# Split activations placed 8 or 16 bytes off a 128-byte line, another place in each stage

## The chip, the cores and the metric

The program runs on one core of one Trainium2 chip. The metric is the device time of one execution in microseconds. A core has TensorE (PE in the profile; its weight loads are shown apart, as PEld), VectorE (DVE), ScalarE (ACT), GpSimd (POOL) and SyncE (SP), which here issues most DMAs.

## The reference

Two transformer blocks run one after the other on 256 tokens of width 1024, all in float32. What is left out below are the gates, masks and scans of each mixer.

```python
def first_block(x, mem, ...):                  # depth 1
    h = h + concat(mlstm(norm(h)), window_attention(norm(h))) @ w_out
    h = h + memory_cross_attention(norm(h), norm(mem), ...)
    h = h + peer_ffn(norm(h), ...)             # 16384 experts, 16 of them per head and token
    return rmsnorm(h, g_final)

def second_block(x, ...):                      # depth 2: even_mixer, then odd_mixer
    h = h + mixer(norm(h))
    h = h + conv_ffn(norm(h))                  # (silu(conv(u)) * v) @ w_down, width 2816
```

The PEER stage is computed here densely: every one of the 16384 experts is multiplied with all tokens, and the coefficients of those not chosen are zero.

## The kernel before

Activations lie feature-major in SBUF: a tile of 128 partitions by 8 blocks of 256 tokens, `[P, 8, T]`. A float32 product is made of three matmuls in the type fp32r. Each operand is split into a high part (`hi`, rounded to fp32r) and a low part (`lo`, what is left), and the sum of high by high, high by low and low by high is accumulated in PSUM (`mm3`, `out_step`). So every matmul of a projection reads a 128x128 block of a weight tile as its stationary operand and 256 tokens of an activation tile, 1024 bytes in each partition, as its moving operand; in `proj_a` the parts are exchanged, and 512 columns of a weight tile are moving.

`weight` brings one weight tile of 512 KB at a time: a DMA on SP into `raw`, `hi` on ACT, `lo` on DVE. The tiles rotate through three to six buffers. One weight tile feeds 24 matmuls of 256 columns: 8 blocks by 3 products.

The stages follow one another: mix (mLSTM and window attention), cross, peer (queries, then 128 tiles of `down`, then 128 tiles of `up` with the coefficients as moving operand), even, ffn0, odd, ffn1. The split activations of a stage come from one of four places:

- `Norm(i)`: the tiles `xh` and `xl` (in the pool `xq`, or `xq2` after the peer stage), or `uh` and `ul` in the pool `xu` for i = 1 (memory) and 3 (peer queries). The 256-column projections read them as moving operand.
- `pair()`: `oh` and `ol`, the input of an output projection in mix, cross, even and odd.
- `peer`: `x.hi` and `x.lo` for the `down` tiles; `u1` for the coefficients of the `up` tiles (`u3` in the program, shown as `u` in the profile).
- `ffn`: `uh` and `ul`, six buffers of 256 tokens each.

Instructions are issued in the order in which the program is recorded; a scheduling layer adds the waits and assigns addresses in the pools. A pool's tiles lie one behind the other, so a pool's start is moved by a small unused tile ahead of it:

```python
    def skip(self, pool, nbytes):
        t = pool.tile([P, nbytes // 4], F32, tag="skip", name="skip", bufs=1)
        self.nc.gpsimd.memset(t, 0.0)
```

In the built program every weight tile (`raw`, `hi`, `lo`) begins at a multiple of 128 bytes. All split activations begin 64 bytes past such a multiple, except those of ffn1 (`Norm(8)`, and `uh`, `ul` of `ffn(1)`), which begin at a multiple.

Of the kernel before, what the change touches and what calls it, by code (L numbers as in the profile page):

```python
# [11 lines left out]
F32R = mybir.dt.float32r  # L12
# [9 lines left out]
P = 128  # L22
T = 256
# [124 lines left out]
    return o  # L148


class Norm:
    early, late = 1, 3

    def __init__(self, b, h, i, pool, tag="x", rpool=None, off=0):
        self.b, self.h = b, h
        self.g = b.g[:, i]
        self.hi, self.lo = [b.placed(pool, F32R, tag + n, off) for n in "hl"]
        self.r = self.R = None
        self.rpool = rpool or b.sp
        self.tag, self.pieces, self.queue = tag, 0, []  # L160
        self.squares = {}
# [211 lines left out]
class Builder:  # L373
# [14 lines left out]
            kw["side"] = side  # L388
        return ctx.enter_context(self.tc.tile_pool(name=name, bufs=bufs, **kw))

    def placed(self, pool, dtype, tag, off):
        if not off:
            return pool.tile([P, 8, T], dtype, tag=tag, name=tag)
        t = pool.tile([P, 8 * T + 32], dtype, tag=tag, name=tag)
        return t[:, off:off + 8 * T].rearrange("p (k t) -> p k t", k=8)

    def skip(self, pool, nbytes):
        t = pool.tile([P, nbytes // 4], F32, tag="skip", name="skip", bufs=1)
        self.nc.gpsimd.memset(t, 0.0)
# [211 lines left out]

    def pair(self):
        o = Pair()
        o.hi = self.op.tile([P, 8, T], F32R, tag=self.ot + "h", name="oh")
        o.lo = self.op.tile([P, 8, T], F32R, tag=self.ot + "l", name="ol")
        return o

    def consts(self, names, arr):
# [29 lines left out]
    def build(self):  # L648
        nc = self.nc
        st = self.stages or ALL  # L650
        last = st[-1]

        def norm(i):
            if i == 3:
                return lambda: Norm(self, self.h, i, self.xu, "u")
            return lambda: Norm(self, self.h, i, self.xq, off=16 if i == 8 else 0)

        def store():
            return Store(self, self.h)

        def final():
            x = Final(self, self.h, self.xq)
            return Finish(self, x) if last == "peer" else x

        self.c = {}
        with ExitStack() as ctx:
            self.sp = self.pool(ctx, "small", bufs=2)
            self.psp = self.pool(ctx, "psum", space=PSUM)
            self.xu = self.pool(ctx, "xu", bufs=1)
            self.skip(self.pool(ctx, "gap"), 64)  # L670
            base = self.pool(ctx, "w0")
            late = ExitStack()
            cq = ExitStack()
            self.skip(self.pool(cq, "gapq", side="right"), 32)
            self.xq = self.pool(cq, "xq", side="right")
            cx = ExitStack()
            self.h = self.pool(cx, "h1", side="right").tile([P, 8, T], F32, tag="h", name="h")
            self.g = self.sp.tile([P, 9, 8], F32, tag="g", name="g", bufs=1)
            self.act_set("silu_and_others")
            nc.scalar.dma_start(self.g, self.A["g_cols"].rearrange("p (i k) -> p i k", i=9))  # L680
            self.ident = self.sp.tile([P, P], F32, tag="ident", name="ident", bufs=1)

            def load_x(i):
                nc.sync.dma_start(self.h[:, 2 * i:2 * i + 2], self.A["x"][:, 2 * i:2 * i + 2])

            load_x(0)
            self.one = self.sp.tile([P, 1], F32, tag="one", name="one", bufs=1)
            nc.vector.memset(self.one, 1.0)
            x = None
            self.wn = 0  # L690
            cw = ExitStack()
            self.wps = [(base, 3), (self.pool(cw, "w1"), 2)]
            with ExitStack() as c1:
                self.cp = self.pool(c1, "c_early")
                self.skip(self.pool(c1, "gapp"), 64)
                self.xp = self.op = self.pool(c1, "xp")
                self.ot = "o"
                if "mix" in st:
                    x = norm(0)()
                    x.split(0)  # L700
                    first = self.weight(self.A["w_in_t"][0], parts=2)
                    for i in range(1, 4):
                        load_x(i)
                        x.split(i)
                    nc.scalar.dma_start(self.ident, self.A["c_ident"])
                    for i in range(4):
                        x.squared(i)
                    x = self.mix(x, first, store if last == "mix" else norm(2))
                else:
                    for i in range(1, 4):  # L710
                        load_x(i)
                    nc.scalar.dma_start(self.ident, self.A["c_ident"])
                if "cross" in st:
                    x = self.cross(x, store if last == "cross" else norm(3), "mix" not in st)
            if "peer" in st:
                x = x or norm(3)().both()
                spill = self.pool(ctx, "spill", space=bass.MemoryType.DRAM).tile([P, 8, T], F32, name="spill")
                x = self.peer(x, base, cw, cx, cq, late, spill, final)
                cx = ExitStack()
                self.wn, self.free = 3, 3  # L720
            else:
                cw.close()
                self.wn = 0
                self.cp = self.pool(late, "c_late", side="right")
                self.consts(LATE, "c_late")
            with ExitStack() as c2:
                self.wps = [(base, 3), (self.pool(c2, "w2"), 3)]
                self.op, self.ot = self.xu, "u"
                if "even" in st:
                    if "peer" not in st:  # L730
                        x = norm(5)().both()
                    x = self.even(x, store if last == "even" else norm(6))
                if "ffn0" in st:
                    x = x or norm(6)().both()
                    x = self.ffn(x, 0, store if last == "ffn0" else norm(7))
                if "odd" in st:
                    x = x or norm(7)().both()
                    x = self.odd(x, store if last == "odd" else norm(8))
                if "ffn1" in st:
                    x = x or norm(8)().both()  # L740
                    self.ffn(x, 1, store)
            late.close()
            cx.close()
            cq.close()
# [336 lines left out]
    def peer(self, xu, base, cw, cx, cq, late, spill, nxt):  # L1081
        nc, A = self.nc, self.A
        mm = nc.tensor.matmul
        with ExitStack() as ctx:
# [1 line left out]
            store = dp.tile([P // 2, P, 2 * T], F32, name="store")  # L1086
            nc.sync.dma_start(spill, self.h)
            x = Pair()
            x.hi = self.xq.tile([P, 8, T], F32R, tag="xh", name="xh")
            x.lo = self.xq.tile([P, 8, T], F32R, tag="xl", name="xl")  # L1090
            work = []
            clock = [0.0, 0.0]

# [33 lines left out]
            for hd in range(8):  # L1127
                before, q = q, rt.tile([P, 2, T], F32, tag="q", name="q")
                for half in range(2):
# [4 lines left out]
                    k = 2 * hd + half - xu.late + 1  # L1134
# [8 lines left out]
            u1 = self.xu.tile([P, 8, T], F32, tag="uh", name="u1")  # L1143
# [80 lines left out]
            nc.sync.dma_start(self.h, spill)  # L1224
            self.cp = self.pool(late, "c_late", side="right")
            self.consts(LATE, "c_late")
            u1 = self.xu.tile([P, 8, T], F32R, tag="uh", name="u3")
            order = [j for j in range(0, P, 2) if j >= kept] + [j for j in range(GA, P, 2) if j < kept]
            order += [j for j in range(0, GA, 2) if j < kept]
            coef = {}  # L1230
# [293 lines left out]
    def ffn(self, x, l, nxt):  # L1524
        nc, A = self.nc, self.A
        with ExitStack() as ctx:
            mp = self.pool(ctx, "ffn%d" % l)
            self.skip(mp, 32 if l else 96)
            mt = self.pool(ctx, "ffnt%d" % l, bufs=6)
            cw = mp.tile([P, FT, 4], F32, name="cw")  # L1530
            nc.sync.dma_start(cw, A["ffn_conv"][l].rearrange("p (f j) -> p f j", j=4))
# [1 line left out]
            def step(f):  # L1533
                u = mt.tile([P, T], F32, tag="u", name="u", bufs=3)

                def ev_u(ps):
                    w = mt.tile([P, T], F32, tag="w", name="w", bufs=2)
                    nc.vector.tensor_mul(w, ps, x.R)
                    nc.scalar.activation(u, w, AF.Identity, scale=cw[:, f, 2:3], bias=cw[:, f, 3:4])
                    for j in (1, 2):  # L1540
                        nc.vector.scalar_tensor_tensor(u[:, j:], w[:, :T - j], cw[:, f, 2 - j:3 - j], u[:, j:],
                                                       op0=ALU.mult, op1=ALU.add)
                    nc.scalar.activation(u, u, AF.Silu)
                    nc.vector.tensor_mul(u, u, x.R)

                self.run(self.proj_b(x, A["ffn_up"][l, f], ev_u, self.tp))
                uh = mt.tile([P, T], F32R, tag="uh", name="uh")
                ul = mt.tile([P, T], F32R, tag="ul", name="ul")

                def ev_v(ps):  # L1550
                    nc.vector.tensor_mul(u, u, ps)
                    self.split(uh, ul, u)

                self.run(self.proj_b(x, A["ffn_up"][l, FT + f], ev_v, self.tp))
                return uh, ul

            after = Lazy(nxt)

            ahead = [step(0), step(1)]

            def steps(f):
# [189 lines left out]
```

## Time and profile before

| | |
|---|---|
| median of 3 runs | 1741.6 us (1729.73 to 1748.4) |
| the profiled execution | 1739.33 us |
| its span, first to last instruction | 1737.6 us |
| PE busy | 1683.0 us, 97% |
| DVE, ACT, POOL busy | 1241.1, 873.8, 89.1 us |

The difference between the profiled execution and its span, 1.7 us, lies outside the instructions. The three runs differ by 1.1%. A busy PE means that at least one matmul was in flight: matmuls overlap, and the profile shows for each a duration that is longer than the distance to the next one. So the rate of the matmuls is read from the distances of their starts, or from how many there are in a stretch.

### The profile page before, as it was taken

Reading aid. Unit: us, or ns where it says so; the run is one execution under the profiler, and the core shown is the slowest. Engines: PE = TensorE matmul, PEld = TensorE weight load, DVE = VectorE, ACT = ScalarE, POOL = GpSimd, SP = SyncE. Lnnn points to the kernel's source line nnn. Section 1 sums busy time; section 2 is a strip of 40 time slices with the busy share of each in tenths; the row PEclk is TensorE's granted clock in tenths of the full one; section 3 lists DMA queues with packets and bytes.
Section 4 is the critical chain, followed back from the end, with each engine's and each line's share of the span. In section 5 each row is a group of like instructions: output and inputs, shape, how many; then the busy total and the mean of one; then the engine's idle time right before and its main releaser. Section 6 shows DMA issues by size and latency. Waiting matters only on the chain.

```text
span 1737.6 us, 33082 instructions
## 1 busy us (share of the span) xinstructions
PE 1683.0 (97%) x13220; PEld 1602.0 (92%) x13220; DVE 1241.1 (71%) x2309; ACT 873.8 (50%) x1358; POOL 89.1 (5%) x246
## 2 busy tenths in 40 slices
PE   7999999999999999999999999899999999999999
PEld 6879889999999999989999999678999987799998
DVE  6686559998798985678555556686777765677775
ACT  6445345545455554444444446464555454455543
POOL 1011010000000000000000000401100010210000
PEclk9999999999999999999999999999999999999999
DMA  7434454577555655889655556443455544345551
GB/s 263 152 104 147 146 172 131 187 236 260 175 186 199 194 196 188 309 289 299 190 189 186 185 189 210 157 135 110 162 192 186 191 159 155 102 162 190 188 188 62
DMA packets 97516, 318.03 MB, mean 183 GB/s; under 512 B 11841, under 2 KB 13505, under 8 KB 96850
## 3 DMA queue, kind: packets, MB, share of 16 engines
q1 hardware_dynamic: 89154, 301.39, 53.1%
q10 hardware_dynamic: 8208, 14.52, 2.2%
q8 instruction: 104, 1.70, 0.4%
q14 instruction: 50, 0.41, 0.1%
HBM read 299.36 MB, written 16.52 MB: 182 GB/s over the span
## 4 chain that ended last, share of the span: by engine, by line
PE 70%; DVE 7%; DMA 3%; POOL 2%; issue 2%; ACT 1%; SPq 0%; POOLq 0%; DVEq 0%; ACTq 0%
PE tp L440 11%; PE tp L441 11%; PE tp L442 11%; PE acc L582 8%; PE acc L583 8%; PE acc L584 8%; PE acc L440 3%; PE acc L441 3%; DMA u<-store 3%; PE acc L442 3%; DVE lo L431 2%; PE tp L1192 1%; PE tp L1193 1%; DVE ga L1244 1%; DVE w L1345 1%
## 5 line engine op out<-in xcount | busy, mean ns | idle before, releaser
L430 ACT ACTIVATE hi<-raw 128x1024 fp32r<-128x1024 f32 (+1 forms) x533 | 560.2, 1057 | 660.8 <-PE tp L441 246.6
L431 DVE TENSOR_TENSOR lo<-raw,hi 128x1024 fp32r<-128x1024 f32 (+1 forms) x533 | 646.7, 1219 | 309.5 <-ACT hi L430 309.2
L440 PE MATMUL tp<-xh,hi 128*128 128x256 f32 x1680 | 476.7, 284 | 0.6 <-ACT u L1207 0.6
L441 PE MATMUL tp<-xl,hi 128*128 128x256 f32 x1680 | 471.8, 281 | 0.0
L442 PE MATMUL tp<-xh,lo 128*128 128x256 f32 x1680 | 471.1, 280 | 0.6 <-DVE lo L431 0.6
L442 PEld LDWEIGHTS tp<-xh,lo 128*128 128x128 f32 x1680 | 317.1, 189 | 0.8 <-DVE lo L431 0.8
L440 PEld LDWEIGHTS tp<-xh,hi 128*128 128x128 f32 x1680 | 317.0, 189 | 0.8 <-ACT u L1207 0.8
L441 PEld LDWEIGHTS tp<-xl,hi 128*128 128x128 f32 x1680 | 317.2, 189 | 0.0
L583 PE MATMUL acc<-u,hi 128*128 128x256 f32 x1024 | 288.4, 282 | 5.6 <-DVE u L436 5.6
L584 PE MATMUL acc<-u,lo 128*128 128x256 f32 x1024 | 288.2, 281 | 1.4 <-DVE lo L431 1.4
L582 PE MATMUL acc<-u,hi 128*128 128x256 f32 x1024 | 287.9, 281 | 0.0
L583 PEld LDWEIGHTS acc<-u,hi 128*128 128x128 f32 x1024 | 193.0, 188 | 6.4 <-DVE u L436 6.4
L584 PEld LDWEIGHTS acc<-u,lo 128*128 128x128 f32 x1024 | 196.9, 192 | 1.8 <-DVE lo L431 1.8
L582 PEld LDWEIGHTS acc<-u,hi 128*128 128x128 f32 x1024 | 193.0, 189 | 0.0
L440 PE MATMUL acc<-hi,xh 128*128 128x512 f32 (+1 forms) x256 | 103.5, 406 | 1.6 <-ACT y L479 1.6
L441 PE MATMUL acc<-lo,xh 128*128 128x512 f32 (+1 forms) x256 | 101.7, 397 | 0.5 <-DVE lo L431 0.5
L442 PE MATMUL acc<-hi,xl 128*128 128x512 f32 (+1 forms) x256 | 101.1, 395 | 0.0
L582 PE MATMUL acc<-uh,hi 128*128 128x256 f32 x352 | 98.3, 280 | 0.1
L583 PE MATMUL acc<-ul,hi 128*128 128x256 f32 x352 | 98.1, 279 | 0.0
L584 PE MATMUL acc<-uh,lo 128*128 128x256 f32 x352 | 98.1, 279 | 0.0
L457 POOL TENSOR_SCALAR rs_g<-rs_m 128x2 int32<-128x2 int32 (+2 forms) x20 | 10.2, 510 | 1263.8 <-DVE fq L296 810.3
L582 PE MATMUL acc<-oh,hi 128*128 128x256 f32 x256 | 73.1, 285 | 0.0
(436 smaller groups left out, 2801.8 us busy)
## 6 DMA issues: line engine op xcount, KB each, us to landing
raw<-down SPq DMA_DIRECT2D x128, 512.0 KB, 3.7
raw<-up SPq DMA_DIRECT2D x128, 512.0 KB, 4.4
raw<-ffn_up SPq DMA_DIRECT2D x88, 512.0 KB, 3.5
raw<-ffn_down SPq DMA_DIRECT2D x44, 512.0 KB, 3.4
raw<-even_in SPq DMA_DIRECT2D x28, 512.0 KB, 4.4
store<-u ACTq DMA_DIRECT2D x55, 256.0 KB, 3.4
u<-store SPq DMA_DIRECT2D x55, 256.0 KB, 4.7
raw<-odd_in SPq DMA_DIRECT2D x24, 512.0 KB, 3.5
```

Of the source, the lines that this page charges most:

```text
L430: nc.scalar.activation(hi[:, c], raw[:, c], AF.Copy)
L431: nc.vector.tensor_sub(lo[:, c], raw[:, c], hi[:, c].bitcast(F32))
L440: mm(out, lh, rh, start=start, stop=False)
L441: mm(out, lh, rl, start=False, stop=False)
L442: mm(out, ll, rh, start=False, stop=stop)
L582: mm(out, wh[:, cs], oh, start=start and j == 0, stop=False)
L583: mm(out, wh[:, cs], ol, start=False, stop=False)
L584: mm(out, wl[:, cs], oh, start=False, stop=stop and j == 1)
L1192: mm(o, p1[:, b, :, e], hi[:, b, :, e], start=True, stop=False)
L1193: mm(o, p1[:, b, :, e], lo[:, b, :, e], start=False, stop=True)
L1244: nc.vector.tensor_mul(src, src, a)
L1345: nc.vector.match_replace(out=w, in_to_replace=val[:, :8], in_values=s, imm_value=-3e38)
```

## The change

A helper `placed` makes a tile with 32 spare elements (128 bytes) and returns the part that begins `at` bytes in. The pools that hold split activations now begin at a multiple of 128 bytes (`xq2` after the peer stage: 64 past one, as before), and a table gives each stage its own place. Weights stay at multiples of 128. The instructions on PE, DVE, ACT and SP are the same in number, shape and order; on GpSimd one memset of a `skip` tile is gone and two have another size.

Since each of the two tiles of a pair is 128 bytes longer, `xl` lies 8320 bytes behind `xh` (8192 before in mix, cross and peer; 8320 before already in the later stages).

What the built program then has for each stage, in bytes past a multiple of 128 (matmuls with 256 moving columns):

| stage | tile | matmuls | before | after |
|---|---|---|---|---|
| mix projections | Norm 0 | 216 | 64 | 56 |
| memory projections | Norm 1 | 192 | 64 | 104 |
| mix and cross output | pair "o" | 384 | 64 | 88 |
| cross queries | Norm 2 | 192 | 64 | 40 |
| peer queries | Norm 3 | 384 | 64 | 24 |
| peer down | x | 3072 | 64 | 16 |
| peer up | u1 | 3072 | 64 | 48 |
| even and odd output | pair "u" | 384 | 64 | 120 |
| ffn0 up | Norm 6 | 1056 | 64 | 80 |
| ffn0 down | uh, ul | 528 | 64 | 112 |
| odd, one tile | Norm 7 | 24 | 64 | 112 |
| ffn1 up | Norm 8 | 1056 | 0 | 72 |
| ffn1 down | uh, ul | 528 | 0 | 8 |

In `proj_a`, where the activations are stationary (816 matmuls with 512 moving weight columns), they begin at 56 (mix), 104 (memory), 80 (even) and 112 (odd) instead of 64. Some float32 tiles of mix and cross move by 64 bytes with their pools.

```diff
+NORM_AT = {0: 56, 1: 104, 2: 40, 3: 24, 5: 16, 6: 16, 7: 48, 8: 8}
+PAIR_AT = {"o": 88, "u": 120}
+EXPERT_AT = 16
+COEF_AT = 48
+FFN_AT = (112, 8)
+LINE = 32
+
+
+def placed(pool, n, dtype, tag, at, **kw):
+    t = pool.tile([P, n + LINE], dtype, tag=tag, name=tag, **kw)
+    return t[:, at // 4:at // 4 + n]
...
-    def __init__(self, b, h, i, pool, tag="x", rpool=None, off=0):
+    def __init__(self, b, h, i, pool, tag="x", rpool=None):
...
-        self.hi, self.lo = [b.placed(pool, F32R, tag + n, off) for n in "hl"]
+        self.hi, self.lo = [placed(pool, 8 * T, F32R, tag + n, NORM_AT[i]).rearrange("p (k t) -> p k t", k=8)
+                            for n in "hl"]
...
-        o.hi = self.op.tile([P, 8, T], F32R, tag=self.ot + "h", name="oh")
-        o.lo = self.op.tile([P, 8, T], F32R, tag=self.ot + "l", name="ol")
+        o.hi, o.lo = [placed(self.op, 8 * T, F32R, self.ot + n, PAIR_AT[self.ot]).rearrange("p (k t) -> p k t", k=8)
+                      for n in "hl"]
...
-            return lambda: Norm(self, self.h, i, self.xq, off=16 if i == 8 else 0)
+            return lambda: Norm(self, self.h, i, self.xq)
...
+            self.skip(self.pool(ctx, "gap"), 64)
             self.xu = self.pool(ctx, "xu", bufs=1)
-            self.skip(self.pool(ctx, "gap"), 64)
...
-            self.skip(self.pool(cq, "gapq", side="right"), 32)
+            self.skip(self.pool(cq, "gapq", side="right"), 96)
...
-                self.skip(self.pool(c1, "gapp"), 64)
...
-            x.hi = self.xq.tile([P, 8, T], F32R, tag="xh", name="xh")
-            x.lo = self.xq.tile([P, 8, T], F32R, tag="xl", name="xl")
+            x.hi, x.lo = [placed(self.xq, 8 * T, F32R, n, EXPERT_AT).rearrange("p (k t) -> p k t", k=8)
+                          for n in ("xh", "xl")]
...
-            u1 = self.xu.tile([P, 8, T], F32R, tag="uh", name="u3")
+            u1 = placed(self.xu, 8 * T, F32R, "uh", COEF_AT).rearrange("p (k t) -> p k t", k=8)
...
-            self.skip(mp, 32 if l else 96)
+            self.skip(mp, 32)
...
-                uh = mt.tile([P, T], F32R, tag="uh", name="uh")
-                ul = mt.tile([P, T], F32R, tag="ul", name="ul")
+                uh, ul = [placed(mt, T, F32R, n, FFN_AT[l]) for n in ("uh", "ul")]
```

## Rows read from the trace of the kernel before

**Rows 1.** The page: span, and busy time of each engine

```profile
span 1737.6 us, 33082 instructions
PE 1683.0 (97%) x13220; PEld 1602.0 (92%) x13220; DVE 1241.1 (71%) x2309; ACT 873.8 (50%) x1358; POOL 89.1 (5%) x246
```

**Rows 2.** Busy time by stretch: peer down, peer up (three), ffn0, ffn1

```profile
core 0: us, PE busy (x) PEld busy (x) DVE busy (x) ACT busy (x) POOL busy (x), PEclk, DMA share, GB/s
302.00:452.00 150.00, 148.75 (x1259) 148.14 (x1258) 139.47 (x454) 76.49 (x115) 0.00 (x0) 1.00 0.66 220
700.00:750.00 50.00, 50.00 (x427) 50.00 (x426) 34.67 (x43) 22.65 (x27) 0.00 (x0) 1.00 0.90 316
750.00:802.00 52.00, 46.95 (x401) 45.92 (x399) 39.94 (x53) 22.03 (x25) 0.00 (x0) 1.00 0.89 301
825.00:1050.00 225.00, 225.00 (x1913) 225.00 (x1912) 121.07 (x121) 105.13 (x120) 0.00 (x0) 1.00 0.60 188
1250.00:1400.00 150.00, 150.00 (x1292) 150.00 (x1291) 109.14 (x164) 77.37 (x109) 0.00 (x0) 1.00 0.58 189
1570.00:1720.00 150.00, 150.00 (x1274) 150.00 (x1273) 107.28 (x161) 75.52 (x107) 0.00 (x0) 1.00 0.52 166
```

**Rows 3.** PE in order of time in peer up, at 900 us

```profile
start us, us, engine line op out<-in xcount [idle before <-releaser]
899.79 0.28 PE L583 MATMUL acc<-u,hi 128*128 128x256 f32 x1
...
900.85 0.28 PE L583 MATMUL acc<-u,hi 128*128 128x256 f32 x1
```

**Rows 4.** PE in order of time in peer up, at 797 us

```profile
796.78 0.28 PE L582 MATMUL acc<-u,hi 128*128 128x256 f32 x1
...
797.46 0.28 PE L582 MATMUL acc<-u,hi 128*128 128x256 f32 x1
```

**Rows 5.** Groups of PE and PEld from 825 to 1050 us (busy us, mean ns)

```profile
L582 PE MATMUL acc<-u,hi 128*128 128x256 f32 x638 | 179.3, 281 | 0.0
L584 PEld LDWEIGHTS acc<-u,lo 128*128 128x128 f32 x638 | 122.5, 192 | 0.0
L582 PEld LDWEIGHTS acc<-u,hi 128*128 128x128 f32 x637 | 119.6, 188 | 0.0
```

**Rows 6.** Groups of PE and PEld from 792 to 800 us

```profile
L582 PE MATMUL acc<-u,hi 128*128 128x256 f32 x24 | 6.6, 276 | 0.0
L584 PEld LDWEIGHTS acc<-u,lo 128*128 128x128 f32 x24 | 4.5, 188 | 0.0
```

**Rows 7.** Groups of PE from 1250 to 1400 us, ffn0: up, then down

```profile
L440 PE MATMUL tp<-xh,hi 128*128 128x256 f32 x294 | 82.5, 281 | 0.0
L582 PE MATMUL acc<-uh,hi 128*128 128x256 f32 x136 | 37.6, 277 | 0.0
```

**Rows 8.** Groups of PE from 1570 to 1720 us, ffn1: up, then down

```profile
L441 PE MATMUL tp<-xl,hi 128*128 128x256 f32 x288 | 81.2, 282 | 0.0
L582 PE MATMUL acc<-uh,hi 128*128 128x256 f32 x137 | 38.4, 280 | 0.0
```

**Rows 9.** Waits, longest first in total, from 700 to 810 us

```profile
ACT hi L430 <- DMA raw<-up: 38.2, 21, 3.1
DVE ga L1244 <- DMA u<-store: 18.3, 13, 2.9
```

**Rows 10.** Float32 matmuls of mix on four places 8 bytes apart, by line (min/median/max ns)

```profile
L865 PE MATMUL tp<-vx,pm x8: 275/275/275, 58.5 to 78.0; 128*128 128x129 f32 x8
```

**Rows 11.** Groups of PE by shape, whole span: 512 moving weight columns

```profile
L442 PE MATMUL acc<-hi,xl 128*128 128x512 f32 x240 | 96.7, 403 | 0.0
L442 PE MATMUL acc<-hi,ul 128*128 128x512 f32 x32 | 12.7, 396 | 0.0
```

More of the change, by code (lines that the diff above doesn't have):

```diff
@@ L389, in pool @@
         return ctx.enter_context(self.tc.tile_pool(name=name, bufs=bufs, **kw))
[L391 to L395, printed above, removed]
     def skip(self, pool, nbytes):
```

## The prediction

> **What bounds the kernel now.** I began with the page's busy shares: PE is busy for 1683.0 of 1737.6 us [rows 1], so nothing on another engine matters unless it holds PE up. Then I cut the span into stretches by stage. In peer up (825 to 1050 us), ffn0 and ffn1 PE has no idle time at all, and in peer down it has 1.25 us of 150; DVE, the next engine, is at 139.47 of 150 there and below three quarters elsewhere, the granted clock is 1.00, its upper level of 2.4 GHz, and the DMA engines are at 0.52 to 0.66 [rows 2]. There the time is the number of matmuls times the distance from one to the next. The exception lies from 700 to about 810 us, where the DMA share is 0.90 and PE loses 5 us in the second of the two stretches, waiting behind weights and reloaded activations [rows 2, 9].
>
> The next view is PE in order of time, read for the distances of starts. At 900 us nine steps take 1.06 us, 117.8 ns each [rows 3]. At 797 us, same line, same tiles, same places, six steps take 0.68 us, 113.3 ns each [rows 4]. 256 columns at 2.4 GHz would take 106.7 ns; 113.3 is 17/16 of that, and 117.8 is another 4.5 ns. So this matmul has **two rates** without any difference in the program. The group views show the same by their means, 281 ns against 276, which tells me how to find the rate of any stage: 276 is the fast one, 281 the slow one [rows 5, 6]. With the slow rate one load of three, that of `lo`, takes 192 ns instead of 188 [rows 5, 6]. The loads of the next block's weights run while a matmul streams, so I read the 4.5 ns as moving operand and weight load getting into each other's way, as a matter of where each stands in its stream when the other begins.
>
> The stages then sort themselves. Peer up is slow except for some 300 matmuls between 757 and 801 us; ffn0 up is slow (281), ffn0 down fast (277), both with activations at 64; ffn1, with activations at 0, is slow in both parts (282 and 280) [rows 5 to 8]. By counts, ffn0 takes 150 us for 1292 matmuls, 116.1 ns, and ffn1 150 us for 1274, 117.7 ns [rows 2].
>
> **The change part by part.** Nothing is added or removed on PE, DVE, ACT or SP, and no wait moves; one small memset less on GpSimd, which is busy 5% [rows 1], costs nothing. What can change is the cost of reading a moving operand that begins elsewhere, and the meeting of the two streams.
>
> Meeting of the streams, best case: every matmul at 113.3 ns. Slow now are the 3072 of peer down, about 2770 of peer up, 1056 of ffn0 up and 1584 of ffn1: 8482 matmuls by 4.5 ns are 38 us. The matmuls from 700 to 750 us (427, 2 us) gain nothing, since DMA at 0.90 is the next limit there; in peer down DVE has 10.5 us left in 150 [rows 2] and the gain is 5.7, so it just fits. That leaves 36 us. The shorter stages of mix, cross, even and odd hold about 1000 more slow matmuls, 4.5 us, mostly hidden under their waits for other engines. The 512-column matmuls of `proj_a`, with the activation as the load, differ by 403 against 396 ns between stages [rows 11]: 816 by 7 ns, at most 6 us.
>
> Meeting of the streams, worst case known: the matmuls that are fast now (528 in ffn0 down, some 300 in peer up, and about 700 in the short stages) fall to the slow rate: 1500 by 4.5 ns, 7 us more.
>
> Which of these holds for the new places no row can say, because the trace has only 64 and 0. What it says is that at 64 both rates occur and a stage keeps the one that it fell into until PE stalls, and that 0 gives no better than the slow one. Twelve different places, 8 or 16 bytes off the ones that are known, most likely give again a mixture. I take the present sum with a little of either end.
>
> A moving operand that begins off an even boundary may also need one more piece read. The nearest row for this is the only one with starts 8 bytes apart: float32 matmuls on `vx`, at four places, take 275 ns at minimum, median and maximum [rows 10]. But a plain float32 matmul runs at half the column rate, so it has slack that an fp32r one has not. I bound the price from below with nothing, by that row. From above: 113.3 ns is 17/16 of the ideal; if this means that data comes in pieces of 64 bytes and each takes 17 cycles instead of 16, then 1024 bytes off a 64-byte boundary touch 17 pieces instead of 16, and a matmul takes 17 by 17 cycles, 289 or 120.4 ns. I take the lower end, by the row, and keep the other as a rival.
>
> ACT and DVE write the split tiles at the new places. That is on no path: from 825 to 1050 us DVE is busy 121.07 us and ACT 105.13 of 225 [rows 2]; they would have to become almost twice as slow before PE waited. In peer down DVE could take 7%.
>
> Sum: the profiled execution is 1739.33 us, 2 us under the median of the three runs; the difference is inside their spread of 1.1%, and I make no correction. With no cost of reading and a mixture of rates as now, from the slow rate everywhere (+7) to a third of the possible gain (-14), the time is 1725 to 1746. I take 1738.
>
> **The rivals.** First, **the mixture stays** (the forecast): 1725 to 1746. For it: both rates occur at one and the same place, so the place alone doesn't choose. Against it: at 0 there is no run of the fast rate as long as those at 64, so the place does matter somewhat.
>
> The Trainium skill goes further: "TensorE: Matmul & The Clock Gate", section "Step-by-step: what each phase is for", says that PE has two independent SBUF read ports, one for the streamed operand and one for the weight loads, and that loading the next weights steals no read bandwidth from the running matmul. By that rule no place would matter, and the time would be the present one, 1739. The trace does not agree in full: a load of 192 instead of 188 ns and a matmul of 281 instead of 276 at the same addresses [rows 5, 6] show that the two do touch.
>
> Second, **the new places take the streams apart**: the fast rate nearly everywhere, 36 us less, with the short stages and `proj_a` up to 45: 1694 to 1703. If half of the large stages get it, about 1720. For it: three quarters of the matmuls are slow now, so there is far more to win than to lose, and a place that is neither 0 nor 64 could shift the meeting for good. Against it: it would have to hold for places as different as 16 and 48 in the two stages that carry most.
>
> Third, **one more piece per matmul**, on the other side: 120.4 ns wherever an activation is the moving operand. The 8482 slow ones lose 2.6 ns each, 22 us, the 1500 fast ones 7.1 ns, 11 us: 1772. It is worth over 1% as soon as about half of the matmuls pay it; were the meeting to come on top (another 4.5 ns), it would go beyond 1800. For it: the 17/16 is there in the fast rate too, where nothing else explains it, so the supply of data is the limit, and a supply limit is what extra pieces would make worse. Against it: 64 and 0 give no hint of a boundary, and pieces may be smaller than 64 bytes. With pieces of 32 bytes there are 33 for 32, 116.9 ns, and the time is within 1% of the present.
>
> "SBUF — State Buffer", section "Specifications (TRN2)", of the Trainium skill gives a line as 16 bytes, with a penalty for each new one. By that only the 8-byte places, 3336 matmuls, touch one line more, 65 for 64, an estimate of 1.8 ns each and 6 us in all: 1745. No run here shows it.
>
> **How the numbers follow.** Chances: the mixture stays 0.45, taken apart in at least half of the large stages 0.26, one more piece 0.29. About 1% is what these runs can tell from no change. Below 1724 lie the second rival and a little of the first: 0.28. Above 1759 lies most of the third: 0.28. Between them is 0.44. The range that leaves out 2 in 10: its lower end at 1704, which keeps the partial forms of the second rival; its upper end at 1776, which keeps the third without the meeting on top.
>
> **What would show it.** In the changed kernel's profile, the distances of starts, or the mean of each group, decide stage by stage: 276 ns in peer down, peer up, ffn0 up and ffn1 would be the second rival; 281 in most and 276 in some, the forecast; about 283 or more in all large stages, the third. If the cost comes from a boundary, the 8-byte stages (ffn1, peer queries) differ from the 16-byte ones (peer, ffn0). DVE and ACT means should stay where they are; if `lo` or the split of an activation grew, that would be a cost that I put at nothing. The forecast is wrong if a single place in peer down or peer up, 3072 matmuls each, moves by more than 6 ns.

## The result: slower by 0.8%

| | before | after |
|---|---|---|
| median of 18 runs | 1734.36 us (1728.44 to 1748.4) | 1749.0 us (1745.21 to 1757.15) |
| the profiled execution | 1739.33 us | 1751.94 us |
| ratio, 95% interval | | 1.0083 (1.0064 to 1.0102) |

The time lies inside the range of the prediction and within 1% of the present one, but on the other side of it: a hair faster was forecast (1738 against 1739.33), and it is measurably slower.

The page of the changed kernel, span and busy times; [rows 1] answer to it:

```profile
span 1750.2 us, 33081 instructions
PE 1699.2 (97%) x13220; PEld 1619.3 (93%) x13220; DVE 1242.1 (71%) x2309; ACT 874.1 (50%) x1358; POOL 88.3 (5%) x245
```

PE is busy 16.2 us longer, the span is 12.6 us longer, so PE is idle 3.6 us less (54.6 us before, 51.0 after): a little of the loss hides in waits for other engines; these are one execution of each kernel. DVE and ACT are the same to 1 us. The two costliest groups of these engines, from the page (engine, operation, names, count, busy us, mean ns):

```profile
L439 ACT ACTIVATE hi<-raw 128x1024 fp32r<-128x1024 f32 (+1 forms) x533 | 560.4, 1057 | 671.3 <-PE tp L450 257.1
L440 DVE TENSOR_TENSOR lo<-raw,hi 128x1024 fp32r<-128x1024 f32 (+1 forms) x533 | 646.5, 1218 | 312.8 <-ACT hi L439 312.5
```

Before they took 1057 and 1219 ns. The whole change is in the rate of PE. By stretch, as [rows 2]:

```profile
302.00:452.00 150.00, 149.39 (x1265) 148.87 (x1264) 140.31 (x460) 76.50 (x117) 0.00 (x0) 1.00 0.68 220
825.00:1050.00 225.00, 225.00 (x1904) 225.00 (x1903) 121.83 (x122) 104.98 (x120) 0.00 (x0) 1.00 0.59 188
1250.00:1400.00 150.00, 150.00 (x1268) 150.00 (x1267) 107.44 (x161) 75.69 (x107) 0.00 (x0) 1.00 0.58 185
1570.00:1720.00 150.00, 150.00 (x1256) 150.00 (x1255) 106.88 (x159) 75.02 (x106) 0.00 (x0) 1.00 0.55 178
```

Peer down counts 1265 matmuls where 1259 stood only because PE is idle less in its window, 0.61 us instead of 1.25; per busy time both give 118.1 ns. In the same time peer up gets 1904 matmuls instead of 1913, ffn0 1268 instead of 1292, ffn1 1256 instead of 1274; a matmul of ffn1 now takes 150 us / 1256 = 119.4 ns, of ffn0 118.3. The granted clock is 1.00 in each, its upper level of 2.4 GHz, as before. Groups of ffn0 from 1250 to 1400 us, up and down, as [rows 7]:

```profile
L449 PE MATMUL tp<-xh,hi 128*128 128x256 f32 x279 | 79.4, 285 | 0.0
L591 PE MATMUL acc<-uh,hi 128*128 128x256 f32 x144 | 40.1, 278 | 0.0
```

285 and 278 ns stand where 281 and 277 stood. The short stages lost most for their size. The output projections read the pair `o`; first its row before, over the whole span (four stages), then after (mix and cross, at 88). Columns: minimum, median and maximum ns, first and last start:

```profile
L582 PE MATMUL acc<-oh,hi x256: 276/276/468, 139.6 to 1538.1; 128*128 128x256 f32 x128
```

```profile
L591 PE MATMUL acc<-oh,hi x128: 278/283/468, 142.1 to 245.4; 128*128 128x256 f32 x128
```

Before, at least half of these matmuls had the shortest duration, 276 ns; now, in mix and cross, none has. From the distances of the starts in the two traces (those under 140 ns, which leaves out the gaps), the mean of each stage is:

| stage | place after | matmuls | before, ns | after, ns |
|---|---|---|---|---|
| memory projections | 104 | 192 | 113.9 | 120.9 |
| mix output | 88 | 192 | 114.4 | 120.3 |
| peer queries | 24 | 384 | 116.8 | 120.7 |
| even output | 120 | 192 | 114.6 | 120.6 |
| ffn1 up | 72 | 1056 | 117.8 | 120.3 |
| ffn1 down | 8 | 528 | 118.4 | 119.2 |
| peer down | 16 | 3072 | 117.7 | 117.9 |
| peer up | 48 | 3072 | 117.3 | 118.3 |
| ffn0 up | 80 | 1056 | 117.7 | 119.7 |
| ffn0 down | 112 | 528 | 113.9 | 116.5 |

What all fp32r matmuls take above 113.3 ns (above twice that with 512 columns), summed in this way, I call the excess: 45.6 us before, 62.8 after. Of the 17.2 us more, 10.1 fall on the stages 8 bytes off a multiple of 16, although these have only 3336 matmuls, and 7.1 on those at multiples of 16. Every mean and every excess here and below comes from one execution.

### The profile page after: what moved, and what is told of

It reads as the page before. It is cut to its first block, busy times and chain, and to the rows that moved or that the text cites. A ratio compares the mean times of both kernels' runs of the same rounds, so it can differ in the third digit from the quotient of the medians.

```text
span 1750.2 us, 33081 instructions
## 1 busy us (share of the span) xinstructions
PE 1699.2 (97%) x13220; PEld 1619.3 (93%) x13220; DVE 1242.1 (71%) x2309; ACT 874.1 (50%) x1358; POOL 88.3 (5%) x245
## 4 chain that ended last, share of the span: by engine, by line
PE 76%; DVE 3%; POOL 2%; DMA 2%; issue 1%; ACT 1%; SPq 0%; POOLq 0%; ACTq 0%; DVEq 0%
PE tp L449 11%; PE tp L451 11%; PE tp L450 11%; PE acc L592 9%; PE acc L591 9%; PE acc L593 9%; PE acc L449 3%; PE acc L450 3%; PE acc L451 3%; DMA u<-store 1%; DVE lo L440 1%; PE tp L1200 1%; PE tp L1201 1%; PE acc L1126 0%; POOL rs_a L469 0%
## 5 line engine op out<-in xcount | busy, mean ns | idle before, releaser
L439 ACT ACTIVATE hi<-raw 128x1024 fp32r<-128x1024 f32 (+1 forms) x533 | 560.4, 1057 | 671.3 <-PE tp L450 257.1
L593 PE MATMUL acc<-uh,lo 128*128 128x256 f32 x1504 | 423.9, 282 | 1.8 <-DVE lo L440 1.8
L591 PE MATMUL acc<-uh,hi 128*128 128x256 f32 x1504 | 424.4, 282 | 0.0
L592 PE MATMUL acc<-uh,hi 128*128 128x256 f32 x1024 | 288.7, 282 | 5.2 <-DVE uh L445 5.2
L593 PEld LDWEIGHTS acc<-uh,lo 128*128 128x128 f32 x1504 | 284.4, 189 | 2.2 <-DVE lo L440 2.2
L591 PEld LDWEIGHTS acc<-uh,hi 128*128 128x128 f32 x1504 | 284.5, 189 | 0.2 <-ACT uh L444 0.2
L592 PEld LDWEIGHTS acc<-uh,hi 128*128 128x128 f32 x1024 | 193.2, 189 | 5.9 <-DVE uh L445 5.8
L592 PE MATMUL acc<-ul,hi 128*128 128x256 f32 x480 | 135.6, 283 | 0.0
L592 PEld LDWEIGHTS acc<-ul,hi 128*128 128x128 f32 x480 | 91.6, 191 | 0.1
L449 PE MATMUL acc<-xh,hi 128*128 128x256 f32 x192 | 58.2, 303 | 8.2 <-ACT xh L186 6.8
L449 PEld LDWEIGHTS acc<-hi,xh 128*128 128x128 f32 x256 | 49.1, 192 | 14.6 <-issue 2.9
```

The costliest lines, as they stand in the source:

```text
L439: nc.scalar.activation(hi[:, c], raw[:, c], AF.Copy)
L449: mm(out, lh, rh, start=start, stop=False)
L591: mm(out, wh[:, cs], oh, start=start and j == 0, stop=False)
L592: mm(out, wh[:, cs], ol, start=False, stop=False)
L593: mm(out, wl[:, cs], oh, start=False, stop=stop and j == 1)
```

## The experiments

Places are in bytes past a multiple of 128 at first, and from the second block of places on in bytes past the weights, modulo 256. Mean distances and the excess are worked out from the starts as above; in the two blocks of extra matmuls the means are those behind the first 24 of each run.

**The places by themselves.** The first kernel adds one block to the kernel before, after its inputs are loaded: for each of 16 places a pair is made and multiplied 144 times; the results are used by nothing, and with 32 weight columns only 32 output partitions are written.

```diff
...
+        for part, w, cols in (("s", wz, 128), ("t", wz, 32), ("r", wm, 128)):
+            for i in range(16):
+                runs(*wu, *wz, 3, 128)
+                at = 2 * i
+                xh, xl = [pp.tile([P, 8 * T + 32], F32R, tag="px" + n, name=part + "abcdefghijklmnop"[i] + n)
+                          for n in "hl"]
+                xh, xl = [v[:, at:at + 8 * T] for v in (xh, xl)]
...
+                runs(xh, xl, *w, 6, cols)
```

> The kernel before, with a block of extra matmuls behind the last store, whose results nothing uses. Each of 48 settings writes a pair of activation tiles at one place (0, 8, ... 120 bytes past a multiple of 128) and runs 144 matmuls of 256 columns in the order of a projection. Part s: weights at 0, loads of 128 columns. Part t: the same with loads of 32 columns and 32 output partitions. Part r: loads of 128 columns, weights at 64. Theory 'meeting' (the weight load and the streamed operand disturb each other, depending on where they begin): in s the steady rate is 113.3 or 117.8 ns at 64 and 118 to 121 ns at places 8 bytes off, in t it is 113.3 ns at every place, and r repeats s with the places shifted by 64. Rival 'one more piece' (a start off a boundary costs the streamed operand by itself): t shows the same surcharge as s at places off the boundary, 2 to 7 ns, and r is as s, unshifted.

Places 0, 8, 16, 24 in part s (weights at 0, 128 columns), then 8 and 16 in part t (32 columns), by tile; the second letter counts the places:

```profile
L768 PE MATMUL acc<-sah,wzh x48: 274/282/415, 1740.5 to 1768.6; 128*128 128x256 f32 x48
L768 PE MATMUL acc<-sbh,wzh x48: 279/283/285, 1777.5 to 1794.4; 128*128 128x256 f32 x48
L768 PE MATMUL acc<-sch,wzh x48: 278/281/286, 1803.4 to 1819.9; 128*128 128x256 f32 x48
L768 PE MATMUL acc<-sdh,wzh x48: 279/286/292, 1828.8 to 1845.9; 128*128 128x256 f32 x48
L768 PE MATMUL acc<-tbh,wzh x48: 283/285/288, 2188.1 to 2205.1; 128*32 128x256 f32 x48
L768 PE MATMUL acc<-tch,wzh x48: 275/278/281, 2214.0 to 2230.3; 128*32 128x256 f32 x48
```

From the first to the last of 48 there are 47 groups of three, 141 steps: 16.9 us at 8 and 17.1 at 24, but 16.5 at 16. Over all 16 places, multiples of 16 take 117.5 ns on average and the others 120.1. With 32 columns all become faster (116.0 at multiples of 16), but 2.9 ns remain between the two kinds. So fewer weight columns relieve the matmul, as the meeting of the streams would have it (though fewer output partitions go with them, and this part can't tell the two apart); the 8-byte surcharge isn't that. With the weights at 64 instead of 0, six of the eight places from 64 on give what the place 64 bytes before gave, to 0.1 ns (72 gives 120.0, as 8 did); the other two and most of those below 64 don't. So the place of the activation against the weights has a part in it, and is not all.

**The whole kernel at one place.** The changed kernel with all places alike; pools and pair distance stay. Shown is 24, and the other two put 64 and 32 everywhere.

```diff
-NORM_AT = {0: 56, 1: 104, 2: 40, 3: 24, 5: 16, 6: 16, 7: 48, 8: 8}
-PAIR_AT = {"o": 88, "u": 120}
-EXPERT_AT = 16
-COEF_AT = 48
-FFN_AT = (112, 8)
+NORM_AT = {0: 24, 1: 24, 2: 24, 3: 24, 5: 88, 6: 88, 7: 88, 8: 88}
+PAIR_AT = {"o": 24, "u": 24}
+EXPERT_AT = 24
+COEF_AT = 24
+FFN_AT = (24, 24)
```

(The tiles of Norm 5 to 8 lie in a pool that begins 64 bytes past a multiple.)

> The changed kernel with every split activation at 64 instead of its own place; the longer tiles (8320 bytes apart) and the moved pools stay. If the places are the cause: back to the kernel before or a little faster, since ffn1 goes from 0 to 64: ratio 0.99 to 1.00. If the longer distance of the two tiles or the moved pools are the cause: as the changed kernel, ratio 1.008.

> The changed kernel with every split activation at 24, an 8-byte place. If 8-byte places cost about 120.5 ns a matmul as in the stages of the changed kernel that have one: 11088 matmuls by 3.5 ns over the mean of before, 39 us less what waits hide, ratio 1.015 to 1.023. If the surcharge of those stages comes from the stages and not from the place: ratio 1.008.

> The changed kernel with every split activation at 32. Theory 'meeting': 32 is neither 0 nor 64 and its rates are open, from 113.3 ns everywhere (ratio 0.977) to 118 ns (1.003). Rival 'one more piece' with pieces of 64 bytes: 120.4 ns, ratio about 1.02; with pieces of 32 bytes: as at 64, ratio 1.00.

| all at | ratio to before, 95% interval | excess, us |
|---|---|---|
| 64 | 1.0048 (1.0017 to 1.0079) | 51.4 |
| 32 | 1.0040 (1.0008 to 1.0073) | 51.3 |
| 24 | 1.0193 (1.0123 to 1.0263) | 81.3 |

24 confirms the surcharge: 120 to 121 ns in every stage. 32 gives 1.0040 and 116.8 to 118.4 ns, where pieces of 64 bytes would have given 120.4 ns and about 1.02. For 64 I was wrong: the old place doesn't bring the old time back. Two things are still different there: tiles and pools lie elsewhere, and the two tiles of a pair are 8320 bytes apart instead of 8192, that is, 128 more than a multiple of 256.

**A period of 256 bytes.** The second block of this kind has pairs 8448 bytes apart (a multiple of 256), and places in steps of 16 over 256 bytes; its part t multiplies with loads of 8 columns, in steps of 8 bytes, and part r has the weights at 8. The results are unused here too, and in t only 8 partitions are written.

```diff
...
-        wm = weights(64, "wm")
-        for part, w, cols in (("s", wz, 128), ("t", wz, 32), ("r", wm, 128)):
+        we = weights(8, "we")
+        for part, w, cols, step in (("s", wz, 128, 4), ("v", wz, 128, 4), ("r", we, 128, 2), ("t", wz, 8, 2)):
...
-                xh, xl = [pp.tile([P, 8 * T + 32], F32R, tag="px" + n, name=part + "abcdefghijklmnop"[i] + n)
-                          for n in "hl"]
+                xh, xl = [pp.tile([P, 8 * T + 64], F32R, tag="px" + n, name=part + letters[i] + n) for n in "hl"]
```

> The kernel before with another block of extra matmuls behind the last store, 64 settings of 144 matmuls of 256 columns; the two tiles of a pair are now 8448 bytes apart, a multiple of 256. Parts s and v (the same twice): weights at 0, loads of 128 columns, places 0, 16, ... 240 past a multiple of 256. Part r: weights at 8, places 0, 8, ... 120. Part t: weights at 0, loads of 8 columns and 8 output partitions, places 0, 8, ... 120. Theory 'streamed operand': an activation that begins 8 bytes off a multiple of 16 costs the streamed operand itself about 2.7 ns; then r has its high rates (120 ns and more) at the same places as before, 8, 24, 40, ..., and t still has a surcharge of 2 to 3 ns there although hardly anything is loaded. Rival 'distance to the weights': in r the high rates move to 0, 16, 32, ..., and t has no surcharge. On the fast rate: in s and v 113.3 ns should occur at 192, where the fast stages of the kernel before stand, and not at 64.

Part s at places 16, 64, 112 and 192, then part t at 8, 16, 24 and 32:

```profile
L769 PE MATMUL acc<-sbh,wzh x48: 278/281/284, 1780.2 to 1796.9; 128*128 128x256 f32 x48
L769 PE MATMUL acc<-seh,wzh x48: 280/280/283, 1857.2 to 1873.8; 128*128 128x256 f32 x48
L769 PE MATMUL acc<-shh,wzh x48: 275/275/284, 1934.6 to 1950.6; 128*128 128x256 f32 x48
L769 PE MATMUL acc<-smh,wzh x48: 276/276/286, 2062.4 to 2078.4; 128*128 128x256 f32 x48
L769 PE MATMUL acc<-tbh,wzh x48: 278/280/283, 3011.6 to 3028.2; 128*8 128x256 f32 x48
L769 PE MATMUL acc<-tch,wzh x48: 275/275/277, 3037.2 to 3053.2; 128*8 128x256 f32 x48
L769 PE MATMUL acc<-tdh,wzh x48: 278/281/285, 3062.2 to 3078.8; 128*8 128x256 f32 x48
L769 PE MATMUL acc<-teh,wzh x48: 276/276/279, 3087.8 to 3103.8; 128*8 128x256 f32 x48
```

In part t, 141 steps take 16.0 us at 16 and 32 and 16.6 at 8 and 24: 113.3 against 117.8 ns, 4.5 ns for 8 bytes with the load practically out of the way. All eight odd multiples of 8 are like that (117.5 to 118.2); of the others six give 113.3 and two, 0 and 96, 116.7. With the weights at 8 the surcharge stays with the activations at odd multiples of 8 (120.0 to 123.7 ns), so it depends on the streamed operand's own address. In part s, with full loads, only 112 and 192 give 113.3 ns; the other 14 places take 117 to 120, and part v, the same once more, repeats all 16 to 0.1 ns. With the weights at 8 the good places are others: 48 and 96 give 113.3 ns (118.3 and 120.0 with the weights at 0), and 112 takes 118.9. Only the weights moved there, so their address has a part in the rate. Place 64 takes 117.8, 128 bytes away from 192: the list doesn't repeat after 128 bytes, the period in which the places were counted so far. Blocks of weights and tokens follow each other by 512 and 1024 bytes, so that all blocks of a tile share their place within 256.

Read in this way, the kernel before falls apart too. Against the weights, both tiles of memory's pair, of the even and odd pair and all buffers of ffn0 are at 192: 113.9 to 114.6 ns. `x` of peer down, the mix projections, the cross queries and cross output are at 64: 117 to 118. Three stages don't fit: mix output, also at 64, with 114.4, and on the other side the peer queries and peer up, which with 3456 matmuls are most of those at 192 and take 116.8 and 117.3 ns. The pair distance of 8320 puts one tile of a pair 128 bytes further on, at 64 instead of 192.

The traces of the two blocks begin with the kernel before at unchanged places, and so show what one place does in other executions. The excess of that part differs by 0.7 us between the three traces, but single stages change their rate: mix output takes 117.2 and 117.8 ns there, and ffn0 down, at 192, 113.5 and 117.7. For ffn0 down in the second block, [rows 7] had 277:

```profile
L582 PE MATMUL acc<-uh,hi 128*128 128x256 f32 x136 | 38.2, 281 | 0.0
```

So 192 allows the fast rate and doesn't ensure it.

**Only multiples of 16; and all at 192.** First the changed kernel with its 8-byte places moved by 8, then one with 256 spare bytes in each tile and every activation 192 bytes from the weights (modulo 256).

```diff
-NORM_AT = {0: 56, 1: 104, 2: 40, 3: 24, 5: 16, 6: 16, 7: 48, 8: 8}
-PAIR_AT = {"o": 88, "u": 120}
+NORM_AT = {0: 48, 1: 112, 2: 48, 3: 16, 5: 16, 6: 16, 7: 48, 8: 16}
+PAIR_AT = {"o": 80, "u": 112}
...
-FFN_AT = (112, 8)
+FFN_AT = (112, 16)
```

```diff
+NORM_AT = {0: 192, 1: 192, 2: 192, 3: 192, 5: 0, 6: 0, 7: 0, 8: 0}
+PAIR_AT = {"o": 192, "u": 192}
+EXPERT_AT = 192
+COEF_AT = 192
+FFN_AT = (64, 64)
+LINE = 64
```

> The changed kernel with its eight places that are not multiples of 16 moved by 8 to ones that are (56 to 48, 104 to 112, 40 to 48, 24 to 16, 72 to 80, 88 to 80, 120 to 112, 8 to 16); those of peer, ffn0 and odd stay. If the 8-byte places are the larger part of the loss: about 3300 matmuls by 2.7 ns are 9 us less than the changed kernel, ratio 1.003 to the kernel before. If the loss is that of the fast rate alone: as the changed kernel, ratio 1.008.

> The changed kernel with every split activation 192 bytes past a multiple of 256 counted from the weights, and 256 spare bytes instead of 128, so that the two tiles of a pair have the same place. If the place within 256 bytes decides whether the fast rate exists (in the kernel before nearly all fast stages stand at 192 with both tiles, the slow ones at 64 or with the tiles at different places): more stages at 113.3 ns, ratio 0.975 to 0.995. If a stage falls into a rate by chance: ratio 0.997 to 1.005.

Without any 8-byte place the ratio is 1.0072 (1.0045 to 1.0098), excess 57.8 us: most of the loss stays, against what I expected. The ratio can't be told from 1.0083; by the traces 5.0 us of the 17.2 come back, all of them in the stages that were moved. Here memory and the pairs hold about 117.8 ns instead of 114, and ffn0 up, at 80, still 119.7. The 8-byte places are a part of the cause, the smaller one. All at 192 is **faster**: 0.9932 (0.9906 to 0.9957), excess 15.1; its trace is of the fastest of its 12 executions (1707.13 us, median 1721.04), so this excess is a low one.

**Distance or place.** Four kernels: the kernel before with pairs 8320 apart and nothing else moved against 128; the changed kernel with pairs at a multiple of 256 and its own places; and all activations at 64 and at 112 of 256, as above with 192. The edit of the first, and the whole of the second's:

```diff
...
-        o.hi = self.op.tile([P, 8, T], F32R, tag=self.ot + "h", name="oh")
-        o.lo = self.op.tile([P, 8, T], F32R, tag=self.ot + "l", name="ol")
+        o.hi, o.lo = [self.placed(self.op, F32R, self.ot + n, 0) for n in "hl"]
...
+            x.hi, x.lo = [self.placed(self.xq, F32R, "x" + n, 0) for n in "hl"]
...
+            u1 = self.placed(self.xu, F32R, "uh", 0)
...
```

(The buffers of ffn0 and ffn1 then lie 1152 bytes apart, so that every other one moves by 128 within 256.)

```diff
-LINE = 32
+LINE = 64
```

> The kernel before with 128 spare bytes in each split tile and nothing else moved: the first tile of each pair stays where it was, the second moves from an even to an odd multiple of 128 bytes behind it (in mix, cross, peer and the outputs; the ffn buffers go 1152 bytes apart instead of 1024). If the distance of the pair is one cause of the loss, the stages that were fast (memory, outputs, ffn0 down) fall to 117.8 ns: 1500 matmuls by 4.5 ns, 5 to 7 us, ratio 1.003 to 1.005. If the places alone count: ratio 1.000.

> The changed kernel with 256 spare bytes in each tile instead of 128, all its places unchanged: the two tiles of a pair stand at the same place of 256 bytes. If the odd distance by itself takes the fast rate away: ratio about 1.003, part of the loss comes back. If the new places have no fast rate anyhow (16 and 48 gave 118.7 and 118.3 ns with pairs at one place in the block of extra matmuls): ratio 1.006 to 1.010, as the changed kernel.

> As the version with every activation at 192 of 256, but at 64, half a period away. If the place within 256 bytes decides: 117.8 ns nearly everywhere, ratio 1.002 to 1.006. If a common place for all tiles was what helped: as at 192, ratio 0.993.

> The same at 112 of 256, the other place where the block of extra matmuls ran at 113.4 ns. If its rates carry over to the stages: ratio 0.98 to 0.995. If a fast rate there depends on how a run begins: between 0.995 and 1.003.

| version | ratio to before, 95% interval | excess, us |
|---|---|---|
| before, pairs 8320 apart | 0.9996 (0.9968 to 1.0024) | 49.3 |
| after, pairs at a multiple of 256 | 1.0066 (1.0038 to 1.0095) | 60.0 |
| all at 64 of 256 | 1.0024 (0.9996 to 1.0051) | 48.5 |
| all at 192 of 256 | 0.9932 (0.9906 to 0.9957) | 15.1 |
| all at 112 of 256 | 0.9886 (0.9847 to 0.9925) | 10.2 |

By the whole time the theory that the distance does it falls: alone it costs nothing that can be measured, and taking it out of the changed kernel leaves 1.0066. By stages it had a point: memory, the outputs of mix, even and odd, and ffn0 down went to 117.7 and 117.8 ns as it said, about 4.5 us, while peer up happened to have more of the fast rate, 24% of its distances under 116 ns instead of 10%. So the places remain, and the distance as far as it puts one tile at another place. The last three differ by nothing but the place within 256 bytes.

The place is not all, either. Peer up at 192 is the example: in the kernel before it got 1913 matmuls in 225 us [rows 2], and in the version with all at 192, at the same place against the weights within 256 bytes,

```profile
825.00:1050.00 225.00, 225.00 (x1988) 225.00 (x1987) 126.73 (x128) 108.25 (x125) 0.00 (x0) 1.00 0.61 195
```

10% and 90% of its distances are under 116 ns. A longer period doesn't explain this: in the built programs peer up of "before, pairs 8320 apart" and of "all at 192" have the same place even within 512 bytes, and 24% and 90%. Read by groups of three starts, peer up changes its rate in these traces at stalls of PE alone: in the first it is fast until the stall at 795 us and slow from there to its end, in the second it is fast from the last stall, at 810 us, to its end. This last stretch has over 2100 matmuls, so by 4.5 ns each its rate alone is worth an estimated 10 us of an execution. Which way a stall turns it is not shown.

**Eight bytes from the best place.** The last kernel moves all activations from 112 to 120 of 256.

```diff
-COEF_AT = 112
+COEF_AT = 120
...
```

> Every split activation moves 8 bytes on from the version with all of them 112 bytes past the weights' multiple of 256, from 112 to 120; the pair distance, the spare bytes and the pools stay. Theory surcharge (a streamed fp32r operand that begins 8 bytes off a multiple of 16 costs each matmul 2.5 to 4.5 ns or more by itself): no matmul at 113.3 ns any more, 118 to 121 ns in all large stages, peer up 1870 to 1910 matmuls in 225 us instead of 1987, and a ratio to the kernel before of 1.008 to 1.02. Theory place alone (only the place within 256 bytes decides, and a neighbour 8 bytes away of a good place is still nearly as good): 113 to 115 ns, ratio 0.985 to 0.997.

1.0187 (1.0123 to 1.0250), excess 81.8 us, median 1766.17 us against 1712.94 at 112 (beside them the kernel before took 1728.24 and 1731.61). Peer up from 825 to 1050 us, at 112:

```profile
825.00:1050.00 225.00, 225.00 (x1987) 225.00 (x1987) 127.26 (x126) 108.90 (x124) 0.00 (x0) 1.00 0.59 195
```

and at 120:

```profile
825.00:1050.00 225.00, 224.78 (x1863) 224.56 (x1862) 124.00 (x126) 103.12 (x117) 0.00 (x0) 1.00 0.58 193
```

1987 matmuls become 1863, 113.2 ns become 120.7, for the same instructions in the same order 8 bytes further on. That is a little more than the surcharge theory gave (1870 to 1910). All at 64 stands between, with 1913 (117.6 ns):

```profile
825.00:1050.00 225.00, 225.00 (x1913) 225.00 (x1912) 121.82 (x120) 105.10 (x120) 0.00 (x0) 1.00 0.56 188
```

The profile of the best version, all at 112, shows where its gain goes:

```profile
span 1709.7 us, 33080 instructions
PE 1649.7 (96%) x13220; PEld 1565.3 (92%) x13220; DVE 1241.5 (73%) x2309; ACT 874.4 (51%) x1358; POOL 89.2 (5%) x245
```

PE is busy 33.3 us less than before, and idle 60.0 us instead of 54.6, so 5.4 us come back as waits; the span is 27.9 us shorter.

## Why the prediction was off

**What bounds the kernel: right.** The rate of PE decides, and nothing on another engine moved. The excess alone gives the ratio: +17.2 us on 1738 is +1.0% (measured 0.83), all at 24 +2.1% (1.93), without 8-byte places +0.7% (0.72), all at 32 +0.3% (0.40). Only towards the faster side does it promise more than arrives, 2.0% against 1.14 at 112, and 1.75% against 0.68 at 192, where the trace is of the fastest execution.

**The price of reading a moving operand that begins elsewhere: this step failed.** I put it at nothing by the `vx` row [rows 10]. That row is right, but it is of a plain float32 matmul, which has time to spare, as I wrote myself; it was the wrong row for an fp32r one (its steps are 109 to 112 ns for 129 columns, where 256 columns in fp32r take 113.3). The price for a start 8 bytes off a multiple of 16 is 4.5 ns with short loads, and 7 ns from the best place in the whole kernel (113.2 to 120.7 in peer up). In the changed kernel the stages with such starts lose 10.1 us over 3336 matmuls, 3.0 ns each. Of these, 5.0 come back when the starts move by 8 bytes to multiples of 16, and that is the price itself here, 1.5 ns each; it is this small because many of the neighbouring places are slow, too (ffn1 up takes 120.3 ns at 72 and 119.8 at 80). The Trainium skill, "SBUF — State Buffer", section "Specifications (TRN2)", has lines of 16 bytes; the measurement agrees that starts off such a line pay. The 1.8 ns estimated from it is too small where nothing else costs (4.5 ns with short loads), and that the estimate of 6 us in all comes near the 5.0 is luck.

**"Most likely give again a mixture": failed too, and this is the larger part.** Without any 8-byte place 12.2 us of the 17.2 are left. I took the two rates for an accident of how a stage begins, since both occur at 64, and carried that over to the new places. But 64 past a multiple of 128 is two places, 64 and 192 of 256, and I had looked at it modulo 128: `u` of peer up and the buffers of ffn0 were at 192, `x` of peer down at 64. All at 64 or all at 192 of 256 are 1.0024 and 0.9932. Half of the step was right: at 192 and at 64 both rates occur, a stretch keeps the one it has and changes at a stall of PE, as peer up at 192 shows ([rows 3, 4] and the traces above), and in the versions with all at 192 and all at 64 peer down has 43% and 37% of its distances under 116 ns. What failed is that the new places would do the same: peer down at 16, peer up at 48 and ffn0 up at 80 have 0%, 0% and 4%, which with ffn0 down makes +7.1 us, and the moved stages lose what fast rate they had. The worst case that I had worked out (+7 for all stages) was too small, since ffn0 up at 80 takes 119.7 ns, more than the 117.8 that I took for the upper rate.

**The rivals.** "Taken apart" exists, at 112 and 192, but not at the new places; its 36 to 45 us for all stages are an excess of 45.6, of which 35.4 go at 112 and 27.9 reach the end. "One more piece" had the right number for the wrong reason: 120.4 ns is what 8-byte places take (120.0 to 121.3 in the large stages of the last experiment), but with pieces of 64 bytes the start at 112 would pay as well, and it takes 113.3. By the rule of two independent read ports ("TensorE: Matmul & The Clock Gate", section "Step-by-step: what each phase is for", of the Trainium skill) the load would not touch the streamed operand. The runs don't agree: in the second block of places, loads of 128 columns give 117.8 to 120.0 ns at 0 to 96 and loads of 8 columns 113.3 at five of these seven, and with full loads the weights' own address changes the rate (118.3 ns at place 48 with the weights at 0, 113.3 with the weights at 8). Nor does that rule speak of where an operand begins, so "no place would matter" didn't follow from it.

**What was to show it.** "Peer down or peer up by more than 6 ns" was too coarse a test: they moved by 0.2 and 1.0 ns (117.7 to 117.9, 117.3 to 118.3), and the loss is spread over all stages. That 8-byte stages would differ from 16-byte ones if the cost is a boundary came true. `proj_a`, at most 6 us, did nothing: its three lines have means of 414, 404 and 402 ns, before 415, 405 and 403. The 192 ns of one load in three were no sign of the upper rate: in peer up of the changed kernel all three take 188, with matmuls of 281 ns:

```profile
L592 PEld LDWEIGHTS acc<-uh,hi 128*128 128x128 f32 x635 | 119.3, 188 | 0.0
L593 PEld LDWEIGHTS acc<-uh,lo 128*128 128x128 f32 x634 | 119.1, 188 | 0.0
```

**What stays open.** Why 112 and 192 of 256 are the good places, and what makes a stretch fast or slow at a place that can hold both rates. The experiments show that the load takes part in it by its address and, unless it is the output that shrinks with it, by its number of columns; they don't show how the two meet.

## What to carry to other kernels

Where back-to-back fp32r matmuls bound a kernel, the start of the moving operand is worth a sweep: keep it at a multiple of 16 bytes, and try places against the weights, since 113.3 and 120.7 ns for the same matmul are 6% of such a stage. Both tiles of a pair can have a good place only if they share it within 256 bytes or it is looked for twice. A place that holds both rates has to be judged by many executions: ffn0 down took 113.5, 113.9 and 117.7 ns in three traces of the same code. Before two rates are put down to chance, compare addresses by a longer period than the one that the code speaks of. A price is read from a row of the same kind of instruction; a row with slack may hide a cost, so it doesn't show that there is none.

## What the runs showed of the hardware that was not expected

- An fp32r matmul of 256 columns takes 4.5 ns more when its moving operand begins 8 bytes off a multiple of 16 (113.3 and 117.8 ns, loads of 8 columns), and 7 ns more in the kernel (113.2 and 120.7).
- With loads of 128 columns its rate depends on the place of the moving operand within 256 bytes: 113.3 ns at 112 and 192, 117 to 120 at the other 14 multiples of 16 (weights at 0, the same in two passes). With the weights at 8 it is 113.3 at 48 and 96, and 118.9 at 112.
- In whole kernels the same place can hold two rates: peer up at 192 of 256 had 10% of its distances under 116 ns in one kernel and 90% in another.
- At multiples of 16 it depends on the number of weight columns, and with them of output partitions, as well: 117.5 ns on average with 128 columns and 116.0 with 32 (pairs 8320 bytes apart).
